# A hybrid decoder layer on one Trainium2 core: first features computed slice by slice, final multiplications in pairs, small matmuls moved

## The chip, the cores and the metric

One core of a Trainium2 chip runs the whole layer in one launch. The metric is the time of an execution on the device in microseconds (us), the median of several runs. Engines are named as the profile names them: PE is the matrix engine (PEld its weight loads), DVE the vector engine, ACT the scalar engine, POOL the GpSimd engine, SP the engine whose queue sends most transfers.

## What is computed

The reference is one decoder layer over 2048 tokens of 1024 features, with 16 learned meta tokens put in front:

```
u = rmsnorm(h, norm_mix_w);  proj = u @ w_in
o_gla = gla_mixer(gq, gk, gv, gr, glr)      # gated linear attention, 4 heads
o_swa = swa_mixer(sq, sk, sv)               # window of 128, sinks, meta keys, 8 heads on 2 key heads
h = h + concat(o_gla, o_swa) @ w_out
h = h + square(relu(rmsnorm(h, norm_ff_w) @ w_ff1)) @ w_ff2
return rmsnorm(h, final_norm_w)[:, 16:]     # meta tokens dropped
```

All is float32. Every large product is made of three matmuls on rounded parts (`mm3`): weight-high by activation-high, weight-low by activation-high, weight-high by activation-low.

## The kernel before

Tokens stand along the free axis, in four blocks of 512 (`NB`); a block's 1024 features are eight tiles of 128 partitions (`KT`). A product of 128 output features for one block (`product`, L162) is 24 matmuls of 128x512 that add up in one PSUM bank.

The layer runs in stages that a Tile scheduler puts in order for each engine; each engine then works its list strictly in order.

- **Constants and warm-up** (`consts` L41, `warm_up` L54): small vectors come by SP's queue; twelve matmuls of 128x128 on ones keep PE busy until data is there.
- **Input projection** (`in_proj` L224), twice, for blocks 0 and 1 and then 2 and 3. `in_prep` (L206) loads x, multiplies by the norm weight and splits it into high (ACT, L153) and low (DVE, L154) parts `u`, and adds squares up for the norm (L88, L91, L92). `split_w` (L117) loads 512 KB of weights and splits them (ACT L123, DVE L124). The first three features (F_Q, F_Q+1 and F_K) are computed for the first block one after the other, each over all eight tiles, then evacuated with the norm factor `rb` (L239 and L241), then for the second block. `rstd_bc` (L94) is the norm factor: a matmul of ones with the squares (`psn`, L97), Ln and Exp on ACT (L79, L80), and three operations on DVE (L81 to L83). `rstd_tok` (L107) makes the same factor once more with tokens on partitions, by eight matmuls of one column (L113). The meta tokens have their own small products (`meta_features` L246, of 48 columns, and one inside `values` L270).
- **Attention** (`swa` L424 and `gla` L633) are two generators. After each `yield` of the dense work, `mix_stage` (L1384) lets each of them go on to its own next `yield`, so that their small matmuls fall between the large ones.
- **Output projection and feed-forward** for blocks 0 and 1 (`trunk`), then for blocks 2 and 3 together with a Strassen-like scheme (`tail_pair`, `tail_ordered`, `Second`).
- **Last stage** (`last_down`, L1322): the last quarter of the second feed-forward product for block 2, then for block 3 in two halves of 256 columns. Each of the eight products of a group is added to the residual by DVE (L1357), squared by ACT and added to `acc` by DVE (L88, L91, L92), and scaled by ACT (L1348). `final` (L1326) makes the norm factor and multiplies each of the eight tiles with it (L1335), six on DVE and two on POOL, and sends pairs out (L1337). It is taken along in steps while the next group is computed. These products use one PSUM pool of three banks, `pd`.

Of the kernel before, what the change touches and what calls it, by code (L numbers as in the profile page):

```python
# [8 lines left out]
F32 = mybir.dt.float32  # L9
# [11 lines left out]
KT = 8  # L21
# [14 lines left out]
class Layer:  # L36
# [16 lines left out]

    def warm_up(self):  # L54

        ps = self.px.tile([P, NB], F32, name="warm", tag="sx")
        for _ in range(12):
            self.nc.tensor.matmul(ps[:, :P], lhsT=self.ones, rhs=self.ones, start=True, stop=True)
# [103 lines left out]
    def product(self, w, act, nk=KT, k0=0, n=NB):  # L162

        wh, wl = w
        ps = self.pd.tile([P, NB], F32, name="psd", tag="d")[:, :n]
# [58 lines left out]
    def in_proj(self, hf, sp):  # L224
# [8 lines left out]
        def weights(f):  # L233
            return self.split_w(a["wf"][f].rearrange("p k c -> p (k c)"))

        def evac(f, nb, ps):
            st = sp.tile([P, NB], F32, name="st", tag="st", bufs=3)
            if F_Q <= f < F_K:
                nc.vector.scalar_tensor_tensor(st, ps, 0.125, rb[nb], ALU.mult, ALU.mult)  # L239
            else:  # L240
                nc.vector.tensor_tensor(st, ps, rb[nb], ALU.mult)  # L241
            if f < F_Q:
                self.rope(sp, st, cs[nb], NB)
            nc.sync.dma_start(out=self.feat[2 * hf + nb, :, f, :], in_=st)

        def meta_features(f, w):  # L246
            wh, wl = w
            ps = self.pd.tile([P, NB], F32, name="psd", tag="d")[:, :48]
            for kt in range(KT):
                c = slice(kt * P, (kt + 1) * P)  # L250
                nc.tensor.matmul(ps, lhsT=wh[:, c], rhs=self.um[kt], start=kt == 0, stop=False)
                nc.tensor.matmul(ps, lhsT=wl[:, c], rhs=self.um[kt], start=False, stop=kt == KT - 1)
            dst = self.m_sk if f == F_SK else self.m_k[:, f - F_K, :]
            nc.vector.tensor_copy(dst, ps[:, 32:48])
            nc.vector.tensor_tensor(dst, dst, ps[:, 0:NM], ALU.add)
            nc.vector.tensor_tensor(dst, dst, self.rbm, ALU.mult)
            if f == F_SK:
                self.rope(sp, dst, self.csm, NM)
# [11 lines left out]
        def values(ch):  # L270
# [4 lines left out]
            if hf == 0:  # L275
                ps = self.pd.tile([P, NB], F32, name="psd", tag="d")[:48, :VH]
                for kt in range(KT):
                    wh, wl = (t[:, (kt % 3) * VH : (kt % 3 + 1) * VH] for t in ws[kt // 3])
                    nc.tensor.matmul(ps, lhsT=self.um[kt], rhs=wh, start=kt == 0, stop=False)
                    nc.tensor.matmul(ps, lhsT=self.um[kt], rhs=wl, start=False, stop=kt == KT - 1)  # L280
                mv = self.m_v[:, ch * VH : (ch + 1) * VH]
                nc.scalar.activation(mv, ps[32:48], AF.Copy)
                nc.vector.tensor_tensor(mv, mv, ps[:NM], ALU.add)
                nc.vector.tensor_scalar(mv, mv, self.rtm, None, ALU.mult)
            for j0 in range(0, 8, 2):
# [12 lines left out]
                for j, ps in zip((j0, j0 + 1), pss):  # L298
                    st = sp.tile([P, NB], F32, name="st", tag="st", bufs=3)[:, :VH]
                    nc.scalar.activation(st, ps, AF.Copy, scale=rt[:, j : j + 1])  # L300
                    nc.sync.dma_start(out=self.vals[8 * hf + j, :, ch * VH : (ch + 1) * VH], in_=st)
                if ch == 1:
                    self.have_v = 8 * hf + j0 + 2
# [3 lines left out]
        ws = [weights(first[0])]  # L307
        prep(0, [lambda f=f: ws.append(weights(f)) for f in first[1:]])
        if hf == 0:
            self.more_consts()  # L310
        pss = []
        for i, f in enumerate(first):
            pss.append((yield from self.product(ws[i], lambda k: u[0][k])))
            if i == 1:
                rb.append(self.rstd_bc(accs[0]))
        for i, f in enumerate(first):
            evac(f, 0, pss[i])
            yield
        prep(1)
        if hf == 0:  # L320
            self.meta_prep(sp)
        for nb in range(2):
            t = sp.tile([P, 2, NB], F32, name="cs", tag="cs", bufs=2)
            nc.sync.dma_start(out=t, in_=a["cs"][2 * hf + nb])
            cs.append(t)
        for i, f in enumerate(first):
            ps = yield from self.product(ws[i], lambda k: u[1][k])
            if i == 0:
                rb.append(self.rstd_bc(accs[1]))
                rt = sp.tile([P, 8], F32, name="rt", tag="rt", bufs=2)  # L330
                self.rstd_tok([accs[j // 4][:, (j % 4) * P : (j % 4 + 1) * P] for j in range(8)], P, rt)
                if hf == 0:
                    self.meta_norm(sp)
            evac(f, 1, ps)
            if hf == 0 and f >= F_K:
                meta_features(f, ws[i])
            yield
        yield from features(F_K + 1)
# [85 lines left out]
    def swa(self, sp):  # L424
# [6 lines left out]
        yield  # L431
        vp, prev = None, None
        nxt = self.swa_prep(0, sp, ld, None)
        for b in range(nblk):
# [128 lines left out]
    def gates(self, gp, lrs, n):  # L563
# [10 lines left out]
        nc.scalar.activation(rows[64:80, :w], ps[:16, :w], AF.Copy)  # L574
        yield
# [422 lines left out]
    def tail_ordered(  # L998
# [316 lines left out]
        hs, hid, ws, rest = W2.run()  # L1315
        for _ in self.last_down(blks, hs, hid, ws, rest):
            pass
# [4 lines left out]
    def last_down(self, blks, hs, hid, ws, rest):  # L1322

        nc = self.nc

        def final(nb, c, acc, last):  # L1326
            n = c.stop - c.start
            rf = self.rstd_bc(acc[:, c], n, last)
            o, k = None, 1024 // n
            for m in range(KT):  # L1330
                h = hs[nb][m][:, c]
                if m % k == 0:
                    o = self.wp.tile([P, 1024], F32, name="o", tag="raw").rearrange("p (k c) -> p k c", k=k)
                eng = nc.gpsimd if m % 4 == 1 else nc.vector
                eng.tensor_tensor(o[:, m % k, :], h, rf, ALU.mult)  # L1335
                if m % 2:
                    nc.sync.dma_start(out=self.out[blks[nb], :, m - 1 : m + 1, c], in_=o[:, m % k - 1 : m % k + 1, :])  # L1337
                yield

        todo = iter(())  # L1340
        for nb, c in [(0, slice(0, NB)), (1, slice(0, 256)), (1, slice(256, NB))]:
            n = c.stop - c.start
            tail, sq = nb == 1 and c.stop == NB, None
# [6 lines left out]
            for m in range(KT):  # L1350
                ps = yield from self.product(ws[m], lambda k: tuple(t[:, c] for t in hid[k][nb]), 4, 0, n)
# [6 lines left out]
                if m == KT - 1 and tail:  # L1358
                    sq = self.np_.tile([P, NB], F32, name="sq", tag="sq", bufs=3)[:, :n]
                    nc.scalar.activation(sq, h, AF.Square)  # L1360
                else:
                    self.sumsq_add(h, acc[:, c], m, n, fast=True)
                if m > 1:
                    weigh(m - 2)
                for _ in range(2 if m > 2 else m):
                    next(todo, None)
                yield
            todo = final(nb, c, acc, sq)
# [24 lines left out]
    def run(self):  # L1393
        tc, nc = self.tc, self.nc
        nc.scalar.preload_act_table_set("natural_log_exp_and_others")
# [6 lines left out]
        with (  # L1402
# [17 lines left out]
            self.warm_up()  # L1420
            with (
# [8 lines left out]
                with tc.tile_pool(name="sa", bufs=1) as sa:  # L1430
                    self.drive(self.in_proj(0, sa))
                    self.drive(self.in_proj(1, sa))
# [21 lines left out]
class Second:  # L1454
# [153 lines left out]
    def run(self):  # L1608
# [36 lines left out]
        return hs, self.hid, self.ws, rest  # L1645
# [13 lines left out]
def layout(inp):  # L1659
# [8 lines left out]
    A["wf"] = np.stack([w[:, c].reshape(KT, P, P).transpose(1, 0, 2) for c in cols])  # L1668
    vc = np.concatenate([np.arange(512, 1024), np.arange(1536, 1552), np.arange(2192, 2320)])
# [49 lines left out]
```

## Time and profile before

| | us |
|---|---|
| median of 3 runs | 2159.56 (2158.14 to 2160.8) |
| the profiled execution | 2160.74 |
| its span, first to last instruction | 2159.0 |
| PE busy | 2135.2 (99%) |
| DVE busy | 1533.2 (71%) |
| ACT busy | 1056.4 (49%) |
| POOL busy | 202.1 (9%) |

The span is cut into 40 equal slices. PE is at nine tenths or more in every slice but the first (8) and the last (7). The granted clock has the digit 9 in all 40. The mean rate of the DMA engines is 135 GB/s, 209 in the first slice. In the chain that ended last PE has 89% of the span, DVE 6%, ACT 3%, DMA 2%.

How to read it: a PE that is busy 99% leaves 23.8 us of the span in which no matmul ran. Matmuls overlap, so the pace is read from the distance between starts and not from the length of one.

### The profile page before, as it was taken

What the parts mean: (1) busy time and instruction counts of PE and PEld (TensorE: products, weight loads), DVE (VectorE), ACT (ScalarE), POOL (GpSimd) and SP (SyncE); (2) the same over time, 40 slices, a digit from 0 to 9 for tenths busy, and PEclk for the clock granted to TensorE, in tenths of its full rate; (3) what the DMA queues carried; (4) which work ended last, traced back from release to release, by engine and by line L of the source; (5) the groups of instructions that cost most, each with busy time, mean ns of one, the idle gap of its engine ahead of it and who ended that gap; (6) DMA issues with size and microseconds to landing.
All of it is one profiled execution on the core that took longest, in us unless ns stands there. A gap on an engine that the chain in (4) does not pass through costs nothing.

```text
span 2159.0 us, 29009 instructions
## 1 busy us (share of the span) xinstructions
PE 2135.2 (99%) x10373; PEld 1798.4 (83%) x10373; DVE 1533.2 (71%) x2848; ACT 1056.4 (49%) x2168; POOL 202.1 (9%) x311
## 2 busy tenths in 40 slices
PE   8999999999999999999999999999999999999997
PEld 6988889888888888888888888888888888888886
DVE  6167774998988887889963445466867776685866
ACT  6132754455765556567652333453545455333434
POOL 2000201122222111212110000000000000000001
PEclk9999999999999999999999999999999999999999
DMA  6334443435333333335333335644345567754412
GB/s 209 96 100 129 142 129 95 124 107 184 104 109 97 113 106 107 106 99 178 120 91 100 95 96 155 199 137 133 126 165 171 171 199 265 276 176 136 156 40 78
DMA packets 150032, 292.51 MB, mean 135 GB/s; under 512 B 14464, under 2 KB 66176, under 8 KB 149888
## 3 DMA queue, kind: packets, MB, share of 16 engines
q1 hardware_dynamic: 149888, 290.66, 42.2%
q8 instruction: 82, 1.34, 0.3%
q14 instruction: 62, 0.51, 0.1%
HBM read 220.68 MB, written 69.86 MB: 135 GB/s over the span
## 4 chain that ended last, share of the span: by engine, by line
PE 89%; DVE 6%; ACT 3%; DMA 2%; issue 1%; SPq 0%; DVEq 0%; ACTq 0%
PE psd L158 16%; PE psd L160 16%; PE psd L159 16%; PE psq L158 4%; PE psq L160 4%; PE psq L159 4%; PE psw L158 4%; PE psw L160 4%; PE psw L159 4%; PE lv L698 2%; PE psd L293 2%; PE psd L294 2%; PE psd L295 2%; PE pv L528 1%; PE kv L616 1%
## 5 line engine op out<-in xcount | busy, mean ns | idle before, releaser
L123 ACT ACTIVATE wh<-raw 128x1024 fp32r<-128x1024 f32 (+2 forms) x190 | 199.4, 1050 | 355.1 <-PE psd L160 318.9
L124 DVE TENSOR_TENSOR wl<-raw,wh 128x1024 fp32r<-128x1024 f32 (+2 forms) x190 | 233.0, 1226 | 72.9 <-ACT wh L123 72.5
L158 PE MATMUL psd<-f,wh 128*128 128x512 f32 x512 | 203.0, 397 | 0.0
L158 PE MATMUL psd<-hid,wh 128*128 128x512 f32 x512 | 202.4, 395 | 0.0
L160 PE MATMUL psd<-f,wh 128*128 128x512 f32 x512 | 199.9, 390 | 0.0
L159 PE MATMUL psd<-f,wl 128*128 128x512 f32 x512 | 199.8, 390 | 0.0
L159 PE MATMUL psd<-hid,wl 128*128 128x512 f32 x512 | 199.7, 390 | 0.0
L160 PE MATMUL psd<-hid,wh 128*128 128x512 f32 x512 | 199.7, 390 | 0.0
L158 PE MATMUL psd<-u,wh 128*128 128x512 f32 x416 | 168.8, 406 | 3.8 <-DVE st L239 2.7
L160 PE MATMUL psd<-u,wh 128*128 128x512 f32 x416 | 165.2, 399 | 0.5 <-DVE u L154 0.3
L159 PE MATMUL psd<-u,wl 128*128 128x512 f32 x416 | 164.2, 395 | 1.0 <-DVE wl L124 1.0
L158 PE MATMUL psw<-bh,wh 128*128 128x512 f32 x392 | 152.5, 389 | 0.0
L159 PE MATMUL psw<-bh,wl 128*128 128x512 f32 x392 | 152.5, 389 | 0.0
L160 PE MATMUL psw<-bl,wh 128*128 128x512 f32 x392 | 152.5, 389 | 0.0
L158 PE MATMUL psq<-oh,wh 128*128 128x512 f32 x384 | 149.8, 390 | 0.0
L160 PE MATMUL psq<-ol,wh 128*128 128x512 f32 x384 | 149.4, 389 | 0.0
L159 PE MATMUL psq<-oh,wl 128*128 128x512 f32 x384 | 149.4, 389 | 0.0
L983 ACT ACTIVATE wh<-rw 128x1024 fp32r<-128x1024 f32 x49 | 52.0, 1061 | 149.2 <-PE psw L160 132.9
L160 PEld LDWEIGHTS psd<-f,wh 128*128 128x128 f32 x512 | 96.1, 188 | 20.7
L160 PEld LDWEIGHTS psd<-hid,wh 128*128 128x128 f32 x512 | 96.1, 188 | 20.6
L158 PEld LDWEIGHTS psd<-hid,wh 128*128 128x128 f32 x512 | 96.2, 188 | 19.2 <-issue 0.2
L159 PEld LDWEIGHTS psd<-hid,wl 128*128 128x128 f32 x512 | 96.2, 188 | 19.1 <-issue 0.2
(321 smaller groups left out, 5152.2 us busy)
## 6 DMA issues: line engine op xcount, KB each, us to landing
raw<-w SPq DMA_DIRECT2D x132, 512.0 KB, 3.6
b<-hops SPq DMA_DIRECT2D x49, 512.0 KB, 3.6
raw<-wo SPq DMA_DIRECT2D x32, 512.0 KB, 3.8
r<-w SPq DMA_DIRECT2D x32, 512.0 KB, 4.2
rw<-w2q SPq DMA_DIRECT2D x28, 512.0 KB, 5.9
raw<-wf SPq DMA_DIRECT2D x26, 512.0 KB, 3.7
feat<-st SPq DMA_DIRECT2D x52, 256.0 KB, 2.0
hops<-t SPq DMA_DIRECT2D x42, 256.0 KB, 5.0
```

What stands on the lines that cost most here:

```text
L123: nc.scalar.activation(wh, raw, AF.Copy)
L124: nc.vector.tensor_tensor(wl, raw, wh.bitcast(F32), ALU.subtract)
L158: nc.tensor.matmul(ps, lhsT=wh, rhs=ah, start=first, stop=False, skip_group_check=skip)
L159: nc.tensor.matmul(ps, lhsT=wl, rhs=ah, start=False, stop=False, skip_group_check=skip)
L160: nc.tensor.matmul(ps, lhsT=wh, rhs=al, start=False, stop=last, skip_group_check=skip)
L293: nc.tensor.matmul(ps, lhsT=ah, rhs=wh, start=kt == 0, stop=False)
L294: nc.tensor.matmul(ps, lhsT=ah, rhs=wl, start=False, stop=False)
L295: nc.tensor.matmul(ps, lhsT=al, rhs=wh, start=False, stop=kt == KT - 1)
L528: nc.tensor.matmul(pv, lhsT=v[:, kv, :], rhs=t, start=i == 0 and t is ph, stop=False)
L616: nc.tensor.matmul(ps[:, hp * 256 : (hp + 1) * 256], lhsT=kT[:, hp * P : (hp + 1) * P], rhs=v[:n, hp * 256 : (hp + 1) * 256], start=True, ...
L698: nc.tensor.matmul(ps[:, hp * P : (hp + 1) * P], lhsT=kl[:, hp, :], rhs=ql[:, :, hp, :], start=True, stop=True)
L983: nc.scalar.activation(wh, src, AF.Copy)
```

## The change

Four things change.

1. **Sliced first features.** For blocks 0 and 1 a new `first_proj` replaces the first part of `in_proj`. The weights of the three first features lie side by side in a new array `w0`, so that one slice of 128 inputs comes with 128x384 numbers. For each slice the three features are advanced together, in three PSUM banks for block 0 and three of a second pool (`pe`) for block 1. The first two slices of weights and the vectors are sent for by ACT's queue; the first tile of x comes in two halves.
2. **Token norms and small matmuls.** `rstd_tok` for tokens is replaced by `token_norms`: the finished `rb` is transposed, four 128x128 tiles for each block, in both passes of `in_proj`. In the first pass what is left (norms, evacuation, meta products) is run by `rest` between the steps of feature F_K+1; the meta product inside `values` stands behind the first pair of value products.
3. **More yields** in `swa` (one ahead of the first `swa_prep`, two behind) and one in `gates`.
4. **Last stage.** Products alternate between two PSUM pools (six banks). The sum of squares of a product is added after the next product's addition (`late`). `final` multiplies two tiles in one DVE operation and uses no POOL. Seven more warm-up matmuls stand ahead of the last norm, whose sum is one matmul.

```diff
-        nc.sync.dma_start(out=t, in_=a["vecs"])
+        nc.scalar.dma_start(out=t, in_=a["vecs"])
...
+    def token_norms(self, rb, sp):
+        rt = sp.tile([P, 8], F32, name="rt", tag="rt", bufs=2)
+        for h in range(2):
+            pt = self.px.tile([P, NB], F32, name="psn", tag="sx")
+            for j in range(4):
+                nc.tensor.transpose(pt[:, j * P : (j + 1) * P], rb[h][:, j * P : (j + 1) * P], self.ident)
+            nc.vector.tensor_copy(rt[:, 4 * h : 4 * h + 4], pt.rearrange("p (a b) -> p a b", a=4)[:, :, 0])
+        return rt
...
+    def first_proj(self, sp, wp, pp):
+        pss = [[pool.tile([P, NB], F32, name="psd", tag=tag) for _ in feats] for pool, tag in ((self.pd, "d"), (pp, "e"))]
...
+        def matmuls(nb, k):
+            for i in range(3):
+                self.mm3(pss[nb][i], *ws[k][i], *u[nb][k], k == 0, k == KT - 1, True)
...
+        for k in range(2):
+            raw[k] = load_w(k, k + 1, nc.scalar)
+            nc.sync.dma_start(out=t[:, k * NB : (k + 1) * NB], in_=src[:, k, :])
+        nc.scalar.preload_act_table_set("natural_log_exp_and_others")
+        self.warm_up()
+        for k in range(2):
+            split_w(raw[k], k)
+            split_x(0, 0, k)
+            matmuls(0, k)
+        for kp in range(1, 4):
+            load_x(0, kp)
+            raw[kp] = load_w(2 * kp, 2 * kp + 2)
+            split_w(raw[kp], 2 * kp)
+            for k in range(2):
+                split_x(0, kp, k)
+                matmuls(0, 2 * kp + k)
+            squares(0, kp - 1)
...
@@ last_down
-            for m in range(KT):
-                h = hs[nb][m][:, c]
-                eng = nc.gpsimd if m % 4 == 1 else nc.vector
-                eng.tensor_tensor(o[:, m % k, :], h, rf, ALU.mult)
+            for m in (0, 1, 4, 5):
+                h = units[nb][m % 2][m // 4].rearrange("p (two c) -> p two c", two=2)[:, :, c]
+                nc.vector.tensor_tensor(o, h, rf.unsqueeze(1).to_broadcast([P, 2, n]), ALU.mult)
+                nc.sync.dma_start(out=self.out[blks[nb], :, m : m + 3 : 2, c], in_=o)
...
-                ps = yield from self.product(ws[m], lambda k: tuple(t[:, c] for t in hid[k][nb]), 4, 0, n)
+                ps = yield from self.product(ws[m], lambda k: tuple(t[:, c] for t in hid[k][nb]), 4, 0, n, pools[m % 2])
...
+                if late:
+                    late()
+                    late = None
...
+                    nc.scalar.activation(sq, h, AF.Square)
+                    late = lambda t=acc[:, c], sq=sq: nc.vector.tensor_tensor(t, t, sq, ALU.add)
...
+            if tail:
+                late()
+                self.warm_up(7)
...
@@ swa
         ld = self.swa_load(0, sp)
         yield
+        yield
         vp, prev = None, None
         nxt = self.swa_prep(0, sp, ld, None)
+        yield
+        yield
```

PE's list at the very start, behind the warm-up; `psd` is an output bank, `u` a tile of x with its two parts, `wh` and `wl` the weights, and the numbers tell buffers apart. Before:

```order
L158 MATMUL psd_213<-u_141,wh_134 128x512
L159 MATMUL psd_213<-u_141,wl_135 128x512
L160 MATMUL psd_213<-u_141,wh_134 128x512
L158 MATMUL psd_213<-u_145,wh_134 128x512
L159 MATMUL psd_213<-u_145,wl_135 128x512
L160 MATMUL psd_213<-u_145,wh_134 128x512
L158 MATMUL psd_238<-u_141,wh_153 128x512
L159 MATMUL psd_238<-u_141,wl_154 128x512
L158 MATMUL psd_213<-u_159,wh_134 128x512
```

Now:

```order
L158 MATMUL psd_97<-u_128,wh_124 128x512
L159 MATMUL psd_97<-u_128,wl_125 128x512
L160 MATMUL psd_97<-u_128,wh_124 128x512
L158 MATMUL psd_98<-u_128,wh_124 128x512
L159 MATMUL psd_98<-u_128,wl_125 128x512
L160 MATMUL psd_98<-u_128,wh_124 128x512
L158 MATMUL psd_99<-u_128,wh_124 128x512
L159 MATMUL psd_99<-u_128,wl_125 128x512
L160 MATMUL psd_99<-u_128,wh_124 128x512
L158 MATMUL psd_97<-u_144,wh_140 128x512
```

Nine matmuls now hang on one tile of x and one slice of weights; before, the first weights (`wh_134`) had to come for all eight slices, and the next three matmuls asked for the next tile of x.

PE's list at the norm of the fourth block, in the second pass of `in_proj`. Before, the eight one-column matmuls follow the norm's at once:

```order
L698 MATMUL lv<-ql,kl_122 128x128 x2
L158 MATMUL psd<-u,wh 128x512
L97 MATMUL psn<-acc,ones 128x512
L113 MATMUL psn<-ones,acc 128x1 x8
L159 MATMUL psd<-u,wl 128x512
```

Now (the ten products left out are of the same kind as the two shown beside the gap):

```order
L97 MATMUL psn<-acc,ones 128x512
L262 MATMUL psn<-tabs,rb 128x128 x4
L818 MATMUL lv<-ql,kl_668 128x128 x2
L159 MATMUL psd<-u,wl 128x512
...
L160 MATMUL psd<-u,wh 128x512
L818 MATMUL lv<-ql,kl_667 128x128 x2
L647 MATMUL pv<-ph,vd 128x512
L262 MATMUL psn<-tabs,rb 128x128 x4
```

The first four transposes read the third block's factor, the second four the fourth block's, which comes of the norm matmul some sixteen instructions ahead.

DVE's list at the very end. Before:

```order
L1357 TENSOR_TENSOR acc<-acc,psd 128x256
L92 TENSOR_TENSOR acc<-acc,sq 128x256
L1357 TENSOR_TENSOR acc<-acc,psd 128x256
L81 SCALAR_TENSOR_TENSOR nt<-psn,ny 128x256
L82 SCALAR_TENSOR_TENSOR nt<-nt,ny 128x256
L83 SCALAR_TENSOR_TENSOR rb<-nt,ny 128x256
L1335 TENSOR_TENSOR o<-acc,rb 128x256 x6
```

Now:

```order
L1476 TENSOR_TENSOR acc<-acc,psd 128x256
L1485 TENSOR_TENSOR acc<-acc,sq 128x256 x2
L1455 TENSOR_TENSOR o<-acc,rb 128x512 x2
L81 SCALAR_TENSOR_TENSOR nt<-psn,ny 128x256
L82 SCALAR_TENSOR_TENSOR nt<-nt,ny 128x256
L83 SCALAR_TENSOR_TENSOR rb<-nt,ny 128x256
L1455 TENSOR_TENSOR o<-acc,rb 128x512 x4
```

Two multiplications of the group before now stand between the last addition and the last norm, and the last six single ones have become four double ones.

## Rows read from the trace of the kernel before

**Rows 1.** Busy time by stretch: PE, PEld, DVE, ACT, POOL; PE clock, DMA share, GB/s.

```profile
6.23:54.00 47.77, 42.45 (x172) 32.15 (x171) 35.28 (x62) 30.64 (x64) 9.95 (x12) 0.93 0.63 208
270.00:290.00 20.00, 19.67 (x97) 16.05 (x96) 16.59 (x37) 11.41 (x28) 1.30 (x2) 0.91 0.44 153
2119.00:2146.00 27.00, 23.33 (x173) 21.15 (x171) 19.50 (x41) 12.01 (x30) 4.78 (x4) 1.00 0.27 105
```

**Rows 2.** Who PE waited for: us in total, times, longest.

```profile
PE psn L97 <- DVE acc L92: 3.2, 3, 2.4
PE psd L158 <- DVE acc L1357: 3.0, 5, 1.4
PE psd L158 <- DVE st L239: 2.7, 1, 2.7
...
PE sc L467 <- DVE qs L413: 0.7, 1, 0.7
```

**Rows 3.** Timeline of the start: start us, us, engine, instruction [idle before <-releaser].

```profile
1.12 5.11 PE L58 MATMUL warm<-ones 128*128 128x128 f32 x24 [1.12 <-DVE ones L48]
...
4.91 1.06 ACT L123 ACTIVATE wh<-raw 128x1024 fp32r<-128x1024 f32 x1 [2.83 <-DMA raw<-wf]
6.00 1.23 DVE L124 TENSOR_TENSOR wl<-raw,wh 128x1024 fp32r<-128x1024 f32 x1 [3.20 <-ACT wh L123]
6.31 0.72 ACT L153 ACTIVATE u<-x,vecs 128x512 fp32r<-128x512 f32 x1 [0.35 <-DMA x<-x]
...
7.09 0.50 PE L158 MATMUL psd<-u,wh 128*128 128x512 f32 x1 [0.86 <-ACT u L153]
```

**Rows 4.** Busy time by stretch, three short ones of the start.

```profile
4.00:5.00 1.00, 1.00 (x7) 1.00 (x6) 0.00 (x0) 0.09 (x1) 0.00 (x0) 1.00 1.08 438
10.00:20.00 10.00, 8.82 (x31) 6.70 (x31) 6.95 (x14) 7.55 (x19) 4.12 (x4) 0.83 0.80 269
34.00:35.00 1.00, 1.00 (x3) 0.76 (x3) 1.00 (x3) 0.63 (x1) 0.00 (x0) 0.50 0.93 295
```

**Rows 5.** Timeline of PE around feature F_K+1.

```profile
53.78 0.18 PE L251 MATMUL psd<-um,wh 128*128 128x48 f32 x1
...
55.49 0.48 PE L158 MATMUL psd<-u,wh 128*128 128x512 f32 x1
...
66.27 0.39 PE L160 MATMUL psd<-u,wh 128*128 128x512 f32 x1
...
68.20 0.33 PE L279 MATMUL psd<-wh,um 128*48 128x328 f32 x1
```

**Rows 6.** Timeline at the norm of the fourth block, PE and DVE.

```profile
275.65 1.12 PE L97 MATMUL psn<-acc,ones 128*128 128x512 f32 x2 [0.33 <-DVE acc L92]
...
276.62 1.84 PE L113 MATMUL psn<-ones,acc 128*128 128x1 f32 x16
...
278.32 0.48 PE L159 MATMUL psd<-u,wl 128*128 128x512 f32 x1
...
280.33 0.67 DVE L83 SCALAR_TENSOR_TENSOR rb<-nt,ny 128x512 f32<-128x512 f32 x1
...
284.91 0.60 PE L508 MATMUL tr<-tabs,p 128*128 128x128 f32 x4
```

**Rows 7.** Timeline of the last stage.

```profile
2120.11 0.28 PE L158 MATMUL psd<-h 128*128 128x256 f32 x1
...
2123.94 0.28 PE L160 MATMUL psd<-l,h 128*128 128x256 f32 x1
...
2145.62 0.28 PE L160 MATMUL psd<-l,h 128*128 128x256 f32 x1
...
2148.18 0.41 DVE L1357 TENSOR_TENSOR acc<-acc,psd 128x256 f32<-128x256 f32 x1
...
2150.23 0.47 ACT L79 ACTIVATE ny<-psn,eps 128x256 f32<-128x256 f32 x1 [0.79 <-PE psn L99]
...
2152.56 3.15 DVE L1335 TENSOR_TENSOR o<-acc,rb 128x256 f32<-128x256 f32 x6
```

More of the change, by code (lines that the diff above doesn't have):

```diff
@@ L52, in consts, with warm_up @@
         self.cp = cp
-    def warm_up(self):
+    def warm_up(self, n=12):
         ps = self.px.tile([P, NB], F32, name="warm", tag="sx")
-        for _ in range(12):
+        for _ in range(n):
             self.nc.tensor.matmul(ps[:, :P], lhsT=self.ones, rhs=self.ones, start=True, stop=True)
@@ L222, in in_prep, with meta_features @@
         return row, acc
-    def in_proj(self, hf, sp):
+    def meta_features(self, f, w, sp):
+        nc = self.nc
+        ps = self.pd.tile([P, NB], F32, name="psd", tag="d")[:, :48]
+        for kt in range(KT):
+            wh, wl = w(kt)
+            nc.tensor.matmul(ps, lhsT=wh, rhs=self.um[kt], start=kt == 0, stop=False)
+            nc.tensor.matmul(ps, lhsT=wl, rhs=self.um[kt], start=False, stop=kt == KT - 1)
+        dst = self.m_sk if f == F_SK else self.m_k[:, f - F_K, :]
+        nc.vector.tensor_copy(dst, ps[:, 32:48])
+        nc.vector.tensor_tensor(dst, dst, ps[:, 0:NM], ALU.add)
+        nc.vector.tensor_tensor(dst, dst, self.rbm, ALU.mult)
+        if f == F_SK:
+            self.rope(sp, dst, self.csm, NM)
@@ new lines, in evac, with load_cs @@
+    def evac(self, blk, f, ps, rb, cs, sp):
+        nc = self.nc
+        st = sp.tile([P, NB], F32, name="st", tag="st", bufs=3)
+        if F_Q <= f < F_K:
+            nc.vector.scalar_tensor_tensor(st, ps, 0.125, rb, ALU.mult, ALU.mult)
+        else:
+            nc.vector.tensor_tensor(st, ps, rb, ALU.mult)
+        if f < F_Q:
+            self.rope(sp, st, cs, NB)
+        nc.sync.dma_start(out=self.feat[blk, :, f, :], in_=st)
+    def load_cs(self, blk, sp):
+        t = sp.tile([P, 2, NB], F32, name="cs", tag="cs", bufs=2)
+        self.nc.sync.dma_start(out=t, in_=self.a["cs"][blk])
+        return t
@@ L225, in in_proj @@
+    def in_proj(self, hf, sp, pools=None):
         nc, a = self.nc, self.a
@@ L236, in evac @@
         def evac(f, nb, ps):
[L237 to L244, printed above, removed]
+            self.evac(2 * hf + nb, f, ps, rb[nb], cs[nb] if cs else None, sp)
         def meta_features(f, w):
             wh, wl = w
[L248 to L258, printed above, removed]
+            self.meta_features(f, lambda k: (wh[:, k * P : (k + 1) * P], wl[:, k * P : (k + 1) * P]), sp)
         def features(f):
@@ L301, in values @@
                     nc.sync.dma_start(out=self.vals[8 * hf + j, :, ch * VH : (ch + 1) * VH], in_=st)
+                if hf == 0 and j0 == 0:
+                    ps = self.pd.tile([P, NB], F32, name="psd", tag="d")[:48, :VH]
+                    for kt in range(KT):
+                        wh, wl = (t[:, (kt % 3) * VH : (kt % 3 + 1) * VH] for t in ws[kt // 3])
+                        nc.tensor.matmul(ps, lhsT=self.um[kt], rhs=wh, start=kt == 0, stop=False)
+                        nc.tensor.matmul(ps, lhsT=self.um[kt], rhs=wl, start=False, stop=kt == KT - 1)
+                    mv = self.m_v[:, ch * VH : (ch + 1) * VH]
+                    nc.scalar.activation(mv, ps[32:48], AF.Copy)
+                    nc.vector.tensor_tensor(mv, mv, ps[:NM], ALU.add)
+                    nc.vector.tensor_scalar(mv, mv, self.rtm, None, ALU.mult)
                 if ch == 1:
@@ L306, in in_proj @@
         first, last = range(F_Q, F_Q + 3), range(NFEAT - 3, NFEAT)
[L307 to L317, printed above, removed]
-            yield
@@ L319, in in_proj @@
[L319 to L337, printed above, removed]
@@ L338, in in_proj @@
-        yield from features(F_K + 1)
+        if pools:
+            u, rb, rest = self.first_proj(sp, *pools)
+            rt = rest(features(F_K + 1))
+            yield
+            cs += [self.load_cs(nb, sp) for nb in range(2)]
+        else:
+            ws = [weights(first[0])]
+            prep(0, [lambda f=f: ws.append(weights(f)) for f in first[1:]])
+            pss = []
+            for i, f in enumerate(first):
+                pss.append((yield from self.product(ws[i], lambda k: u[0][k])))
+                if i == 1:
+                    rb.append(self.rstd_bc(accs[0]))
+            for i, f in enumerate(first):
+                evac(f, 0, pss[i])
+                yield
+            prep(1)
+            cs += [self.load_cs(2 * hf + nb, sp) for nb in range(2)]
+            for i, f in enumerate(first):
+                ps = yield from self.product(ws[i], lambda k: u[1][k])
+                if i == 0:
+                    rb.append(self.rstd_bc(accs[1]))
+                    rt = self.token_norms(rb, sp)
+                evac(f, 1, ps)
+                yield
@@ L339, in in_proj @@
+        if hf:
+            yield from features(F_K + 1)
         yield from values(0)
@@ L1419, in run @@
             self.consts(cp)
-            self.warm_up()
+            left = contextlib.ExitStack()
+            sa = left.enter_context(tc.tile_pool(name="sa", bufs=1, side="right"))
+            with (
+                tc.tile_pool(name="w0", bufs=1) as w0,
+                tc.tile_pool(name="pe", bufs=3, space=PSUM) as pe,
+            ):
+                first = self.in_proj(0, sa, (w0, pe))
+                next(first)
             with (
@@ L1429, in run @@
                 self.streams = [self.gla(gp), self.swa(sp)]
-                with tc.tile_pool(name="sa", bufs=1) as sa:
-                    self.drive(self.in_proj(0, sa))
+                with left:
+                    self.drive(first)
                     self.drive(self.in_proj(1, sa))
```

120 lines of the change are left out of this document (89 added, 31 removed).

## The prediction

> **What bounds the kernel now.** I read the page first: PE runs matmuls in all but 23.8 us of the span of 2159.0, so whatever else is saved has to show up as a shorter list for PE, as less waiting, or as a shorter piece ahead of PE's first or behind its last product. Then I read busy time by stretch, to find where the 23.8 us lie [rows 1]. The stretch from 6.23 to 54.00, in which the first three features are made for blocks 0 and 1, has 5.3 us without a matmul and a mean granted clock of 0.93. The last stage from 2119 to 2146 has 3.7 us. Two more pieces lie at the ends, 6.2 us before and 13 us behind. Nearly all of the middle is dense; the exception that this change touches is 270 to 290, where the clock is 0.91. Third, the list of PE's waits [rows 2] says on whom: on sums of squares (3.2 us), on the residual additions of the last stage that free its banks (3.0), on one evacuation (2.7, at the start, three banks for three features) and on the first window attention (0.7). Last I read the timelines of those places [rows 3, 5 to 7].
>
> At the start the order is the cause. The first product hangs on 512 KB of weights, which are there at 4.91, and on x at 6.31; the first real matmul starts at 7.09, 0.86 us after the warm-up has ended [rows 3]. Then PE waits for tile after tile, and after such waits the granted clock falls to 0.50, 1.2 in place of 2.4 GHz, for some three microseconds, as in 34 to 35 [rows 4].
>
> **The first features, sliced.** I compare both kernels at one place: the end of the meta product of feature F_K+1, at 68.20 before [rows 5]. Up to there both have the same 192 large matmuls, two norms and two meta products on PE. What the new list needs:
>
> - The warm-up is unchanged and ends at 1.12 + 5.11 = 6.23 [rows 3]. The first slice (0.46 MB in place of 1 MB) is due ahead of that: 512 KB were there at 4.91 [rows 3]. So the first product starts at 6.23.
> - 192 matmuls. From 55.49 to 66.27 PE made 47 steps [rows 5], 0.229 us each, so 44.0.
> - Two norm matmuls, 275.65 to 276.62 [rows 6], 0.97 each: 1.9.
> - Eight transposes: four took 0.60 [rows 6], so 1.2. They are new here; the sixteen one-column instructions go.
> - The meta tokens' own norm matmuls are in both lists; I put in 0.6, as for one such small group.
> - Two meta products, 53.78 to 55.49 [rows 5], 1.71 each: 3.4.
>
> That is 57.4. The feeders: a slice asks PE for 9 x 0.229 = 2.06 us. ACT needs for it a split of 384 weight columns and of x and a square; by 1.06 for 1024 columns and 0.72 for 512 [rows 3], some 0.4 + 0.7 + 0.7 = 1.8. DVE needs by 1.23 for 1024 columns [rows 3] some 0.5 + 0.7 + 0.7 = 1.9. Both fit, narrowly, and both begin a microsecond ahead of PE. In ACT's and DVE's lists the squares stand behind the splits of the next slices, so they are not in the way. The second block asks for less (no weights), and the norm of the first block, its three evacuations (0.7 each) and the meta preparation go into that slack; their cover is the three further banks, without which the 2.7 us of [rows 2] would come back.
>
> Transfers: a slice is 0.46 MB each 2.06 us, 223 GB/s. From 10 to 20 the engines moved 269 [rows 4]. Slices 3 and 4 come as one pair of transfers, 0.92 MB; behind 0.92 MB that are there by some 5.8 us, at 269 GB/s they land at 9.2, are split by 11.0, and PE asks at 10.4. I charge 0.6 us. Would the second queue spare it? From 4 to 5 us a single queue already moved 438 GB/s with the sixteen engines full (share 1.08) [rows 4], so what is sent by ACT takes its share from x, and I credit the queue with nothing. The Trainium skill, "DMA: Bandwidth & Descriptors", "Issuing engines are not separate DMA queues", speaks against this part in the same way: transfers issued from several engines interleave on the same 16 DMA engines, and only the issuing time is saved. If it were not so, the 0.6 us would go and the sum below would be 20.5.
>
> So the place is reached at 58.0, **10.2 us earlier**. Ends: 11.4 with no wait and the transposes half hidden, 6 in the first rival.
>
> **The second pass.** The sixteen one-column instructions take 276.62 to 278.32, 1.7 us [rows 6]; eight transposes take 1.2: 0.5 gained. Behind them the clock is low: 0.91 over 20 us is 1.8 us of PE's time [rows 1]. I take this as gained, since the idle and the 1.7 us of tiny matmuls ahead of it go. New is a wait: the second four transposes need the fourth block's factor. Before, it was finished at 281.00, 4.4 us after the norm matmul [rows 6]; in the new list four transposes, eleven large matmuls and two or three small groups lie between, 0.6 + 2.5 + 0.8 = 3.9. PE waits 0.5, and with it everything behind, for PE's list is strict. Nearest rows for its other end: 2.4, the longest wait for a sum of squares [rows 2]. The additional yields move the first scores of the window attention away from the preparation that they waited 0.7 us for [rows 2]; I take 0.3. Groups of small matmuls in the middle become 206 in place of 208, which I cost at nothing; the bounds are a microsecond either way. **2.1 us** in all, between -3 and +4.
>
> **The last stage.** 2120.11 is the start of the 28th of the 192 matmuls of 256 columns; from there to 2123.94 are 32 steps, 0.120 us each [rows 7]. At that pace the last one, 164 further, starts at 2139.7, with half a norm matmul (0.5) between at 2140.2. It started at 2145.62 [rows 7]: 5.4 us went to waits for banks and to the refilling of the pipeline. With six banks DVE may fall behind by five products. Its own work in these two groups: 31 additions of 0.41 [rows 7], two norms (2.0 and 1.2), four double multiplications of 1.23, as for 1024 columns [rows 3], and two of 0.67: 22.2 us against PE's 24.4. What made DVE late before, waiting for ACT's square in each product, goes with the later addition. I take 5.2 of the 5.4.
>
> Behind the last matmul (2145.90) 4.3 us passed until Ln at 2150.23 [rows 7], since DVE was a product behind. Now the addition starts some 0.2 after it; addition to Ln took 2.05, one more addition of 0.45 stands between, and the norm matmul, kept from the low clock by the seven warm-ups, gives back 0.4: 2.3. Saved: 2.0. From Ln to the first multiplication nothing changes. The multiplications took 3.15 [rows 7] and take 4 x 0.67 = 2.7: 0.4. The two that stand ahead of the last norm lie under ACT's Ln and Exp. **7.6 us**; ends 4 (double cost of the broadcast operand, half of the waits) and 8.5.
>
> **Sum.** 10.2 + 2.1 + 7.6 = 19.9 from the profiled execution's 2160.74 gives 2140.8. That execution is 1.2 above the median of the runs, 2159.56, so I predict **2139.7** for the median.
>
> **Rivals.**
>
> 1. The slices come late. At the mean rate of that stretch, 208 GB/s [rows 1], a slice takes 2.2 us and PE waits at each of the first eight, 1.1 us, and some 1 more at the third; the clock falls once for 1.8. 2143.6. For: 269 is a rate of an emptier PE. Against: 438 early on [rows 4].
> 2. The wait for the transposes in the second pass is the long one, 2.4, and brings the low clock again, 1.8, for DVE is full there. About 2143.4.
> 3. Transposes bring the low clock as the one-column matmuls did: 1.8 not gained and 1.8 more in the first pass. 2143.3.
> 4. A multiplication with a repeated operand takes 1.23 for 512 columns: 2.2 more at the end and some 2 of waiting inside. 2143.9.
> 5. Slower. ACT and DVE use 1.8 and 1.9 of 2.06 us in each slice. If every handover costs a little more, PE idles in every slice, and the granted clock stays at the half that is seen behind such gaps [rows 4]. At half speed each of 144 matmuls costs 0.23 more, 33 us; 2172. It decides from 87 of the 144, where the gain of 19.9 is used up. Against: before, with much longer gaps, only stretches of some three microseconds were slow.
>
> **How the numbers follow.** My case 0.55, rivals 1 to 5 0.13, 0.11, 0.10, 0.08 and 0.03. Only the fifth is slower; two of the others together with the bad ends can eat most of the gain. A measurement of this kernel tells 0.2%, 4.3 us, from no change: faster 0.95, same 0.02, slower 0.03. The range goes down to the three good ends together, 11.4 + 4 + 8.5 = 23.9 of gain, 2135.7, and some way below for a middle that gains more than I count, 2134; upwards to two of the rivals 1 to 4 together, 2147.
>
> **What would show it.** Right: a first product at about 6.2 and no clock below 1.00 up to 60 us; meta product of F_K+1 done near 58; the bank waits of the last stage (3.0 us) gone; some 10.5 us from the last product to the end of the span. Wrong: PE waiting for `wl` or `u` in every slice, or for `rb` in front of the transposes, or a last stage in which the residual addition is still what PE waits for.

## The result and the profile after

| | before | after |
|---|---|---|
| median of four runs (the three named above and one more), us | 2160.18 (2158.14 to 2160.82) | 2146.65 (2146.13 to 2147.08) |
| the profiled execution | 2160.74 | 2146.13 |
| its span | 2159.0 | 2144.4 |

The ratio is 0.9939, with an interval of 0.9922 to 0.9956: 13.5 us faster by the medians, 14.6 by the two profiled executions. The forecast was 19.9; the time lies 7 us above the predicted one, at the upper end of the range.

I cut both traces at two places that both kernels pass: the end of the meta product of F_K+1, and the first product of the last stage. The second cut of before is this row of PE's timeline:

```profile
2094.26 0.39 PE L158 MATMUL psd<-h 128*128 128x512 f32 x1
```

| stretch | before | after | change | forecast |
|---|---|---|---|---|
| start to the meta product of F_K+1 | 68.20 | 58.63 | -9.6 | -10.2 |
| from there to the last stage | 2026.06 | 2028.99 | **+2.9** | -2.1 |
| last stage to the end | 64.74 | 56.78 | -8.0 | -7.6 |

Two of three terms came out; the middle has the other sign. The timeline of PE after, from the first product to the value products, answers to [rows 3, 5]:

```profile
6.63 0.50 PE L158 MATMUL psd<-u,wh 128*128 128x512 f32 x1 [1.02 <-ACT u L153]
...
48.06 0.60 PE L262 MATMUL psn<-tabs,rb 128*128 128x128 f32 x4
...
49.10 0.66 PE L262 MATMUL psn<-tabs,rb 128*128 128x128 f32 x4
...
55.14 0.18 PE L230 MATMUL psd<-um,wh 128*128 128x48 f32 x1
...
58.63 0.40 PE L404 MATMUL psd<-wh,u 128*128 128x328 f32 x1
...
59.30 0.47 PE L404 MATMUL psd<-wh,u 128*128 128x328 f32 x1
59.57 0.47 PE L405 MATMUL psd<-wl,u 128*128 128x328 f32 x1
...
62.51 0.31 PE L404 MATMUL psd<-wh,u 128*128 128x328 f32 x1
62.66 0.31 PE L405 MATMUL psd<-wl,u 128*128 128x328 f32 x1
```

The transposes wait for nothing. The two meta products stand in one piece, 55.14 to 58.63, and behind them the value products start 0.27 us apart and then, from 62.51, 0.15. Busy time by stretch after, with the columns of [rows 1]:

```profile
6.63:49.10 42.47, 42.18 (x178) 32.67 (x178) 34.01 (x57) 29.23 (x58) 2.41 (x7) 1.00 0.65 227
58.63:62.51 3.88, 3.88 (x17) 3.88 (x17) 1.78 (x5) 1.36 (x3) 0.91 (x3) 0.56 0.76 208
260.00:280.00 20.00, 19.67 (x101) 15.57 (x100) 19.66 (x45) 13.53 (x36) 5.89 (x8) 1.00 0.31 104
2087.00:2134.00 47.00, 47.00 (x298) 42.52 (x297) 34.02 (x61) 22.02 (x47) 0.00 (x0) 1.00 0.13 51
```

The sliced stage is dense at the full clock. The clock of 0.56 in the second row is new: most of that stretch ran at 1.2 GHz, and by the steps (0.27 in place of 0.15) it cost 1.5 us. The clock of 0.91 in the second pass [rows 1] is gone, and so is the idle of the last stage. Whom PE waited for after, against [rows 2]:

```profile
PE lr L689 <- issue: 1.1, 1, 1.1
PE lr L689 <- DVE S L892: 1.1, 1, 1.1
PE warm L58 <- DVE ones L48: 1.1, 1, 1.1
PE lv L818 <- DVE AT L823: 1.1, 1, 1.1
PE psd L158 <- ACT u L153: 1.0, 1, 1.0
PE pv L647 <- DVE pl L631: 0.9, 1, 0.9
PE sc L586 <- DVE nt L81: 0.5, 1, 0.5
```

Of the groups on the list of before that the change aimed at, only the first scores still wait (`sc`, 0.5 in place of 0.7, for other work). Four waits of the attention of about 1 us each are new. From the first value product to the end of the attention PE idles 5.4 us, counting waits of 0.15 us and more; before it was 1.7. The tail, PE, ACT and DVE, against [rows 7]:

```profile
2087.62 0.39 PE L158 MATMUL psd<-h 128*128 128x512 f32 x1
...
2133.70 0.28 PE L160 MATMUL psd<-l,h 128*128 128x256 f32 x1
...
2134.96 0.43 DVE L1485 TENSOR_TENSOR acc<-acc,sq 128x256 f32<-128x256 f32 x1 [0.18 <-ACT sq L1484]
2135.30 1.28 DVE L1455 TENSOR_TENSOR o<-acc,rb 128x512 f32<-128x512 f32 x2
...
2138.51 2.50 DVE L1455 TENSOR_TENSOR o<-acc,rb 128x512 f32<-128x512 f32 x4
```

From first to last product 46.1 us (before 51.4), from the last to the end 10.7 (before 13.4). A multiplication with the repeated operand takes 0.64 here, so the fourth rival is out.

### The profile page after: what moved, and what is told of

It reads as the page before. It is cut to its first block, busy times and chain, and to the rows that moved or that the text cites. A ratio compares the mean times of both kernels' runs of the same rounds, so it can differ in the third digit from the quotient of the medians.

```text
span 2144.4 us, 28980 instructions
## 1 busy us (share of the span) xinstructions
PE 2127.4 (99%) x10369; PEld 1795.4 (84%) x10369; DVE 1532.7 (71%) x2848; ACT 1050.6 (49%) x2166; POOL 181.1 (8%) x300
## 4 chain that ended last, share of the span: by engine, by line
PE 89%; DVE 6%; ACT 2%; DMA 2%; issue 1%; POOL 0%; DVEq 0%; ACTq 0%; SPq 0%; POOLq 0%
PE psd L158 16%; PE psd L160 16%; PE psd L159 16%; PE psq L158 4%; PE psq L159 4%; PE psq L160 4%; PE psw L159 4%; PE psw L158 4%; PE psw L160 4%; PE lv L818 2%; PE psd L404 2%; PE psd L405 2%; PE psd L406 2%; PE pv L647 1%; DMA x<-x 1%
```

## The experiments

Each kernel was timed beside the kernel before on one chip, in three sessions; "against before" is the difference to the median of before in its session. The stretches are cut as above.

| kernel | median | ratio to before | against before | first stage | middle | last stage |
|---|---|---|---|---|---|---|
| no_yields | 2141.80 | 0.9904 to 0.9932 | -17.9 | 59.44 | 2024.34 | 56.8 |
| no_gate_yield | 2146.34 | 0.9923 to 0.9948 | -13.3 | 58.54 | 2029.26 | 56.8 |
| no_swa_yields | 2144.93 | 0.9922 to 0.9946 | -14.7 | 58.65 | 2028.64 | 57.6 |
| meta_apart | 2145.37 | 0.9923 to 0.9948 | -14.3 | 58.73 | 2028.11 | 56.8 |
| before_yields | 2163.43 | 1.0009 to 1.0026 | +4.2 | 68.71 | 2028.57 | 64.3 |
| before_tail | 2151.72 | 0.9948 to 0.9975 | -7.5 | 68.16 | 2025.30 | 56.7 |
| sp_queue | 2142.04 | 0.9904 to 0.9931 | -17.2 | 58.53 | 2025.37 | 56.8 |
| both | 2140.18 | 0.9896 to 0.9923 | -19.0 | 58.05 | 2023.77 | 56.8 |
| one_column | 2141.73 | 0.9911 to 0.9938 | -16.5 | 58.95 | 2024.18 | 56.8 |
| three_banks | 2141.71 | 0.9910 to 0.9935 | -16.5 | 58.27 | 2023.38 | 58.0 |
| meta_thrice | 2145.35 | 0.9930 to 0.9954 | -12.9 | 61.01 | 2025.82 | 56.8 |
| first_gate | 2139.39 | 0.9898 to 0.9925 | -18.8 | 58.86 | 2021.97 | 57.0 |

### The added yields

**no_yields**, the changed kernel without part 3:

```diff
         ld = self.swa_load(0, sp)
         yield
-        yield
         vp, prev = None, None
         nxt = self.swa_prep(0, sp, ld, None)
-        yield
-        yield
...
         nc.scalar.activation(rows[64:80, :w], ps[:16, :w], AF.Copy)
         yield
-        yield
```

> The changed kernel without its four added yields (three in swa, one in gates). In the changed kernel PE waits 5.4 us between the first value product and the end of the attention, 1.7 in the kernel before over the same work. Theory A, the yields moved the small matmuls ahead of the DVE work that they need: the waits fall back to about 1.7 and the execution from 2146.1 to about 2142.4. Theory B, the waits come from the new first pass and its other number of steps: they stay near 5.4, 2146. Theory C, the yields pay for themselves: the late waits go, but the first scores and the last steps wait as long in their place, 2145 to 2147.

2141.8: theory A. No run of this kernel is above 2144.2, none of the change is below 2146.1, in two sessions whose medians of before differ by 0.5. The idle of the attention falls from 5.4 to 2.5 us, 2.9 of the 4.7 by which the middle is shorter. Another 1.5 of it is the low clock behind the meta products, which this trace doesn't have (below), so the yields alone account for some 3 of the gain and not for all of it. What a yield does is seen at the end of the fourth GLA chunk. `lr` transposes into one of two PSUM banks, the one in which `kv` stands until DVE has made the state `S` from it. The change, timeline of PE and DVE:

```profile
415.12 1.02 PE L736 MATMUL kv<-v,kT 128*128 128x256 f32 x4
...
416.47 0.68 DVE L245 TENSOR_TENSOR st<-psd,rb 128x512 f32<-128x512 f32 x1
417.07 0.33 DVE L892 SCALAR_TENSOR_TENSOR S<-S,eB,kv 64x128 f32<-64x128 f32 x1
...
418.45 0.69 DVE L203 TENSOR_TENSOR sw<-sw,cs 128x512 f32<-128x512 f32 x1
...
418.73 0.60 PE L909 MATMUL oT<-tabs,o 128*128 128x128 f32 x4
...
420.89 0.35 DVE L892 SCALAR_TENSOR_TENSOR S<-S,eB,kv 64x128 f32<-64x128 f32 x1
...
421.39 0.38 PE L689 MATMUL lr<-tabs,lr 128*16 128x128 f32 x2 [1.13 <-DVE S L892]
```

Without the yields, the same chunk:

```profile
416.18 1.42 DVE L888 SCALAR_TENSOR_TENSOR S<-S,eB,kv 64x128 f32<-64x128 f32 x4
...
417.96 0.60 PE L905 MATMUL oT<-tabs,o 128*128 128x128 f32 x4
...
418.39 0.38 PE L686 MATMUL lr<-tabs,lr 128*16 128x128 f32 x2
```

Some steps later, `kv` falls together with the evacuation and rotation of a feature, the four updates of `S` are mixed into that chain, and the last ends 4.2 us after the first began instead of 1.42. In PE's list `lr` comes four matmuls behind `oT`, and PE stands for 1.13 us until the last update is done. The wait at 1016 is of the same kind: DVE's reading of `lv` (0.72 at 1015.19) stands behind a split of weights of 1.23.

**no_gate_yield** and **no_swa_yields**: the same edit, one half of it each.

> The changed kernel without the yield added in gates, the three of swa kept. The four waits that look like gates' (421, 970, 1016 and 1026 us, 4.3 in sum) stand behind it. Theory A with the gates' yield as the cause: these go, some 1.1 to 1.5 us of waiting is left, about 2142. Theory A with the yields of swa as the cause: little changes, 2145 to 2146. Theory B: nothing changes, 2146.

> The changed kernel without the three yields added in swa, the one in gates kept. If gates' yield alone makes the late waits, they stay, and the 0.7 us that the first scores waited before comes back: 2146 to 2147. If it is the distance between both streams that matters, the waits change in number and place: anything from 2142 to 2148. Theory B: 2146.

Neither half is the culprit alone. Without gates' yield the four waits that I had put down to it are gone, and others of the same sum stand in their place (1.5 and 1.1 us for `oT`, 1.6 in three waits for `z`): 5.6 us of idle, no gain. Without those of swa 3.7 us are left. My two expectations for a single cause were wrong. That it matters at which dense step each group falls, as the expectation for no_swa_yields allowed, fits all four kernels; it is read from the rows at two of the waits, and argued for the others.

**before_yields**, the kernel before with the four yields and nothing else:

> The kernel before with the four yields alone added. Theory A, the yields themselves put the small matmuls ahead of the DVE work that they need, whatever the first pass does: PE's waits from the first value product to the end of the attention go from 1.7 us to about 5, the time up by 3 to 4 us, some 2163. Theory B2, they hurt only together with the new first pass: 1.7 us of waiting, 2159 to 2160.

4.2 us slower, theory A again. The waits of its attention are those of the change, at the same steps of the work, under other line numbers:

```profile
PE lr L573 <- DVE S L776: 1.1, 1, 1.1
...
PE lv L702 <- DVE AT L707: 1.1, 1, 1.1
PE lr L573 <- PE oT L793: 1.0, 1, 1.0
PE pv L531 <- DVE pl L515: 0.9, 1, 0.9
PE sc L470 <- DVE nt L81: 0.8, 1, 0.8
```

The idle of its attention is 5.6 us, 3.8 more than before. So the new first pass isn't needed for it. The middle is only 2.5 us longer, since the low clock of [rows 1] at 270 to 290 isn't in this trace (1.00 in place of 0.91).

### The low clock behind the meta products

**meta_apart** puts the meta product of F_K between the third and the last quarter of F_K+1:

```diff
             self.meta_norm(sp)
-            next(nxt)
             self.meta_features(F_K, lambda k: ws[k][2], sp)
+            next(nxt)
             for _ in nxt:
```

**both** is this edit and no_yields together. **meta_thrice** is no_yields with `meta_features(F_K)` called twice in a row, so one product is made once more than needed.

> The changed kernel with the meta product of F_K put between the third and the last quarter of feature F_K+1, so that twelve large matmuls stand between the two meta products, which now follow each other in one piece of 3.5 us. Theory D, this one piece brings the low clock of 59 to 62 us: the values' first products run at 0.15 us a step in place of 0.27, 1.5 us less, 2144.6. Rival: two meta products bring it wherever they stand that near to each other: still a low clock, 2146.1, perhaps earlier by 2.7 us.

> The changed kernel without the four yields and with the meta product of F_K put apart. Joined meta products were followed by the low clock in three kernels (1.2 to 2.5 us) and not in the fourth, the one without yields; apart there was none in one look. Theory D: none here either, and the value products start at about 58.7 and run at 0.15; against the kernel without yields nothing to 1 us better, 2140.8 to 2141.8. Rival, the fall has nothing to do with the meta products: it shows here too, 1 to 2 us slower.

> The changed kernel without the four yields (2141.8, span 2140.6, joined meta products, no low clock in its one look), and the meta product of F_K made twice in a row, so that three stand in one piece of 5.2 us. The third costs 1.75 us of its own. Theory D, the piece of small matmuls brings the low clock: it falls, for 1.5 to 4 us' worth, span 2143.8 to 2146. Rival, the fall has nothing to do with the piece: the span is 2142.4 and the values run at 0.15 us a step from the start.

The first four microseconds of the value products, busy time by stretch, of no_yields (joined), both (apart) and meta_thrice (three joined):

```profile
59.44:63.40 3.96, 3.96 (x28) 3.96 (x28) 1.79 (x5) 1.37 (x3) 0.91 (x3) 1.00 0.75 213
```

```profile
58.05:62.00 3.95, 3.95 (x28) 3.95 (x28) 1.36 (x4) 0.75 (x1) 1.42 (x2) 1.00 0.68 204
```

```profile
61.01:65.40 4.39, 4.39 (x17) 4.39 (x18) 1.84 (x5) 1.36 (x3) 1.18 (x2) 0.50 0.49 138
```

With two or three joined the clock fell in five of six profiled kernels: 0.56 after the change, 0.60 without gates' yield, 0.50 without swa's, 0.57 in sp_queue, 0.50 in meta_thrice, where the last ten matmuls of the third product already lie 0.21 apart in place of 0.11. By the steps that cost 1.5 us in three of them and 3.1 in no_swa_yields and meta_thrice. Only no_yields kept 1.00. Apart it stayed 1.00 in all five kernels (meta_apart, both, one_column, three_banks, first_gate).

The mean clock of every execution says the same, though it can't tell where a fall lies: it is 0.999 in 6 of the 28 executions with the products joined, lower in the other 22, and 0.999 in 18 of the 23 with them apart. It also suggests that one kernel does both. no_gate_yield took 2144.4 us in its two executions at 0.999 and 2146.3 to 2146.7 in its three at 0.998; of no_yields the slowest, 2144.13, has 0.997. So the joined piece brings the fall, in most executions and, as far as these means tell, not in all; what decides it in one of them is open.

meta_thrice's profiled span, 2143.6, lies 0.2 under the range that I gave. meta_apart by itself is 1.3 us below the change in median, with overlapping ranges, since its waits at `lr` came out 0.6 longer; both is 1.6 below no_yields, in another session, and 1.9 below sp_queue, in its own session and with the fall; I had expected 0 to 1 against the one trace without it.

### The queue

**sp_queue**: from no_yields, `nc.scalar` becomes `nc.sync` for the vectors and for the first two slices of weights.

> The changed kernel without the four yields (span 2140.6, first product at 6.34 there), and with the vectors and the first two slices of weights sent for by SP's queue again. Prediction's theory, the queue is worth nothing: first product at 6.2 to 6.9, as in the five kernels with ACT's queue (6.34 to 6.99), time within 1 us of 2141.8. Rival, the issues behind each other on one queue delay the first half of x by two issues of 0.43: first product at 7.2 or later, the gaps of the first two slices longer, 1 to 2 us slower.

2142.04 against 2141.8: worth nothing, as forecast, but not because nothing moves. Timeline of ACT and PE with one queue:

```profile
3.77 0.52 ACT L290 ACTIVATE wh<-raw 128x384 fp32r<-128x384 f32 x1 [1.69 <-DMA raw<-w]
...
5.44 0.50 PE L158 MATMUL psd<-u,wh 128*128 128x512 f32 x1
...
11.69 0.96 PE L158 MATMUL psd<-u,wh 128*128 128x512 f32 x3 [1.00 <-ACT wh L290]
```

The same split with two queues, in the change:

```profile
5.45 0.52 ACT L290 ACTIVATE wh<-raw 128x384 fp32r<-128x384 f32 x1 [1.95 <-DMA raw<-w]
```

Both kernels send for the first slice of weights at some 1.25 us. With one queue it can be split at 3.77, with two, where x's tiles are sent for at the same time, at 5.45. The first product starts at 5.44, earlier than in any kernel with ACT's queue (6.34 to 7.39), and PE then waits for the third slice. The place is reached at 58.53, against 59.44 in no_yields and 58.54 to 58.65 in the three other kernels with the same first pass and two queues. My range for the first product, 6.2 to 6.9, and the rival's, 7.2 or later, were both wrong. The Trainium skill, "DMA: Bandwidth & Descriptors", "Issuing engines are not separate DMA queues", says that only issuing time is to be saved by a second engine; by that rule the times should be alike, and the two medians agree.

### The last stage

**before_tail**: part 4 alone on the kernel before. **three_banks**: both, with the products in `pd` alone:

```diff
-        pools = ((self.pd, "d"), (pq, "q"))
+        pools = ((self.pd, "d"), (self.pd, "d"))
```

> The kernel before with the new last stage alone (two pools, later addition of squares, paired multiplications, seven warm-ups). If its gain stands by itself: from the first product of the last stage to the end 56.8 us in place of 64.7, time 8.0 lower, about 2151.6. Rival: a part of it comes with the other changes: less than 6, 2154.

> The same base (2140.2), and all products of the last stage in the one pool of three banks again; the later addition of squares, the paired multiplications and the seven warm-ups stay. If the banks gave the 5.3 us that went from the waits of the last stage: PE waits 3 to 5 us there again, 2143 to 2145. Rival, the later addition alone had made DVE fast enough: less than 1 us of waiting, 2140 to 2141.

The stage gains by itself what it gains in the change: 64.74 to 56.74, and 7.5 us by the medians where I expected 8.0. With three banks it takes 57.95, 1.2 us more and not 3 to 5. No single wait is long enough to be listed; the loss stands in four places alike, of which this is one, timeline of DVE and PE:

```profile
2113.26 1.22 DVE L1451 TENSOR_TENSOR o<-acc,rb 128x1024 f32<-128x1024 f32 x1
...
2114.39 0.42 DVE L1472 TENSOR_TENSOR acc<-acc,psd 128x256 f32<-128x256 f32 x1
2114.47 0.28 PE L160 MATMUL psd<-l,h 128*128 128x256 f32 x1
...
2114.86 0.39 PE L158 MATMUL psd<-h 128*128 128x256 f32 x1
```

The addition that frees the bank stands behind a double multiplication of 1.22, and two starts of PE lie 0.39 apart in place of 0.12. With six banks the same place is dense. So with the other parts in place the three further banks are worth 1.2 of the 5.3 us; the later addition and the paired multiplications take away the other 4 without them. No run takes these two apart, has the banks alone, or leaves out the seven warm-ups.

### The second pass

**one_column**: both, with the sixteen one-column matmuls in the second pass again (`rstd_tok` for `token_norms`).

> The changed kernel without the four yields and with the meta product apart (2140.2, span 2138.6), and in its second pass the sixteen one-column matmuls with their own norm again in place of the transposes. Prediction's term: one-column matmuls 1.7 us for 0.8, and the low clock behind them, which cost 1.4 to 1.6 in the kernel before, comes back: 2.3 us slower, 2142.5. Rival, the low clock there came from the wait for the squares alone: only 0.9 slower, 2141.1. Rival 2, the norm of its own lets the value products start earlier, for rb is not waited for: no slower, 2140.

I had expected 2.3 us; by the medians it is 1.5, in another session. The middle is 0.4 us longer than in both; the first stage is 0.9 longer, 0.6 of it by a later first product (7.39 for 6.80), with which this edit has nothing to do. In this trace the one-column piece brings no low clock, although PE waited 0.29 us for the squares ahead of it as it did before (0.33), as the timeline and the busy time of the stretch behind it show:

```profile
267.16 1.84 PE L113 MATMUL psn<-ones,acc 128*128 128x1 f32 x16
```

```profile
267.00:287.00 20.00, 20.00 (x108) 16.95 (x107) 16.36 (x35) 9.55 (x24) 2.98 (x4) 1.00 0.38 119
```

With one-column matmuls the clock fell there in before and before_tail (0.91 both), and not in before_yields and one_column; with transposes in none of ten kernels. The four other executions of one_column have a mean clock of 0.998 for the 0.999 of the profiled one, so this may differ between executions too. What lets it fall there is open; the gain of some 1.6 us, ten steps of before from 278.32 that took 3.96 in place of 2.3, was real in this pair of traces, but it isn't had each time.

### A better version

**first_gate**: both, and gates' second yield for the meta tokens' gates alone (`if m == 1: yield`).

> The base without the four yields and with the meta product apart (2140.2), and the gates' added yield back for the meta tokens' gates alone, where PE waits 0.78 for ACT's row parts (z at 116.6). If a yield can be had without harm there: 0.8 us less, 2139.4. Theory A, all later steps of gla stand one step later against swa and the dense work: waits of 0.5 to 1.1 may come in other places, 2139.4 to 2142.

The wait for `z` is gone and nothing has come in its place; the waits that are left, from 0.3 us up:

```profile
PE warm L58 <- DVE ones L48: 1.1, 1, 1.1
PE psq L158 <- DVE cc L1404: 0.5, 1, 0.5
PE oT L907 <- DVE o L880: 0.5, 1, 0.5
PE psn L97 <- DVE acc L92: 0.3, 1, 0.3
PE psd L158 <- ACT u L153: 0.3, 1, 0.3
```

The idle of the attention is 1.0 us, the span 2137.8, the shortest of all. By the ratios it can't be told from both (0.9912 and 0.9910, in two sessions). Both beat the change by some 5 us against before (19.0 and 18.8 for 13.5).

## Why the prediction was right and wrong

The two profiled executions lie 14.6 us apart where I forecast 19.9. Of the 5.3 that are missing, 5.0 are in the middle.

**The first features: right.** 10.2 forecast, 9.6 measured: 58.0 against 58.63 and, in both, 58.05. The start was later than I had it (6.63 for 6.23, on ACT's part of x, 1.02 of waiting). Behind it the sum came out within 0.3, partly by luck: the transposes took 0.8 by their starts and not 1.2, for I had added up the lengths of matmuls that overlap, while the steps, waits and refilling took some 0.9 more than my 44.0 and 0.6. Neither late slices (rival 1) nor the half clock (rival 5) came. The sign "no clock below 1.00 up to 60 us" failed, at 59 us, by the meta products.

**The last stage: right in size** (7.6 for 8.0), and its parts too: 5.3 for 5.2 up to the last product, 2.7 for 2.4 behind it. That the waits went "for banks" was the weaker half of the cause: in three_banks only 1.2 us come back.

**The second pass and the middle: wrong, 2.1 gained for 2.9 lost.** What I costed by rows came out in sum: in both, without the two items below, the middle is 2.3 us shorter than before. The parts were less exact: the transposes take 0.8 by their starts where the one-column matmuls took 1.7, so 0.9 was gained for 0.5 forecast (0.4 in the middle of one_column); the low clock behind them was worth 1.6 for 1.8; and the wait of 0.5 for `rb` did not come (rivals 2 and 3 out). Two steps failed:

- "The additional yields move the first scores of the window attention away from the preparation that they waited 0.7 us for; I take 0.3." I looked at the one wait that the yields were next to. They shift later small groups against the dense work, swa's by three steps, gla's by one at each of the nine calls of `gates`. Price: 3.4 us of idle between both and the change, 3.8 alone on the kernel before.
- "Groups of small matmuls in the middle become 206 in place of 208, which I cost at nothing." That counts groups and forgets what joining makes: 32 matmuls of 48 columns without a large one between, and the low clock behind them. Price: 1.5 us in this trace.

The two are 4.9 of the 5.0 us by which the middle missed. The bound of -3 for this term just held the loss, but the grounds that I gave for it were a long wait for the transposes (2.4) and a microsecond for the small groups, and no rival stood for the yields. That the time lies inside the range is luck: its upper end stood for two of the rivals 1 to 4 together, and none of the four came.

**The queue at nothing: right in the time**, by sp_queue; the first slice moved by a microsecond and more, which I hadn't seen coming.

## What to carry to other kernels

Where streams are woven into dense work by counted steps, one more step anywhere is a change everywhere behind it: cost it by asking, at every later group, what stands in the other engines' lists at the new step, or try it alone. Joining small groups can cost more than it saves when it makes one long piece; here it paid to keep large matmuls between such pieces. And ask of a wait whether the engine that is late can be relieved: here that took away some 4 us of waits with three banks, and three further banks 1.2 more.

## What the runs showed of the hardware

- The clock fell behind a piece of matmuls in which PE was never idle: 32 of 48 columns in 3.5 us, then 0.56 (1.2 GHz for most of the next 3.9 us). In before I had seen it fall only behind waits and one-column matmuls. With twelve large matmuls between two pieces of 16 it fell in none of five kernels.
- The same piece need not do it: 1.00 in one of six, and executions of one kernel differ (no_gate_yield 2144.4 us at a mean clock of 0.999, 2146.3 to 2146.7 at 0.998). One trace of a low clock gives no price.
- In one trace with one queue the first slice came earlier than in ten with two: first product at 5.44, against 6.34 to 7.39, and the weights' split at 3.77, against 5.45 in the change.
